# Stick-breaking and differential attention on one core: V and gate columns of the stick-breaking heads computed by seven products ahead of attention, heads reordered and overlapped

## The chip, the core and the metric

The kernel runs on one core of a Trainium2 chip. A core has a matrix engine (TensorE, PE in the profile; PEld is its weight load, which overlaps the products), a vector engine (VectorE, DVE), an activation engine (ScalarE, ACT), GpSimd (POOL) and SyncE (SP), which mostly issues transfers. Each engine runs its own instructions in order and waits for others by semaphores. Operands lie in SBUF (128 partitions), results of TensorE in PSUM. The metric is the device time of one execution in microseconds (us).

## The reference

One layer over 1024 tokens of 2048 features, batch 1:

```python
hn = rmsnorm(h, norm_mix_g[i])
proj = hn @ w_in[i]                              # 2048 x 8192
sb_q, sb_k, sb_v, sb_g, df_q, df_k, df_v, df_g = jnp.split(proj, split_at, axis=-1)
# 8 stick-breaking heads of 128, per query block:
z = q @ k.T * scale;  mask = kpos < qpos
log_not_beta = where(mask, -softplus(z), 0)
later = cumsum(log_not_beta, reverse=True) - log_not_beta
w = where(mask, exp(log_sigmoid(z) + later), 0);  sb_out = w @ v
# 8 differential heads: two 64-wide q/k pairs with partial rotary, one V of 128
a = softmax1 - lam * softmax2;  df_out = rmsnorm(a @ v) * (1 - lambda_init)
mixed = concatenate([sb_out * silu(sb_g), df_out * silu(df_g)])
h = h + mixed @ w_out[i]
gate = sigmoid(rmsnorm(h, norm_ple_g[i]) @ w_ple_gate[i])
h = h + gate * (p[i] @ w_ple_proj[i])
return rmsnorm(h, norm_final_g)
```

All of it is float32, and every product in the kernel keeps nearly float32 precision by three products of rounded halves (fp32r): high by high, high by low, low by high (lines L220, L221, L222).

## The kernel before

Activations lie transposed: features on the 128 partitions, tokens along the free dimension, in reversed order, so that a causal row is a contiguous range and the reverse cumulative product of stick-breaking becomes a forward scan (L313). The tokens are worked in two halves of 512, `half` 1 first (the earlier tokens, whose queries see only that half's keys), then half 0, whose queries see the keys of both. K and V of half 1 go to DRAM (`k_d`, `v_d`) and come back in half 0.

**A unit.** `unit(X)` multiplies two blocks of 128 columns of `w_in` with 16 feature tiles of the half: 2 x 16 x 3 = 96 matmuls of 128x512, into two PSUM tiles `acc`. Its weights come in four pieces; for each, ACT writes the high part (`whi`, L150) and DVE the low part (`wlo`, L151), two pieces deep. A head needs two units: q and k, then V and gate. So half 1 has 32 units, half 0 too.

**The order of the work.** TensorE's instructions are ordered by hand. A head's attention is cut into steps with due times, and `Side.tick()`, called after each group of three matmuls (32 ticks to a unit), issues the steps that are due between the matmuls of the units that follow. Thus attention of one head lies in the units of the next one. The steps of a stick-breaking head: `weights(rb)` for four blocks of 128 queries (scores on TensorE, mask on DVE L300, two sigmoids on ACT L311 and L312, scan L313 and product L314 on DVE, which give the weights `bt`); `values` (transposes of V, `vps`, L336); then, for two pairs of query blocks, `turn` (transposes of the weights into `tp`, L352, split into `awh` on ACT L364 and `awl` on DVE L365) and `mix` (weights by V into `av`, L380 to L385, reduced at L390 and L391). The order of ACT and DVE is chosen by the framework's scheduler in the heads; in the seven-product stage it is written by hand as well.

**PSUM.** Tag "t" has two buffers for `tp`, `vps`, `av` and the small norm sums; tag "acc" two; tag "z" two buffers of two banks for scores.

**The order of heads.** In half 1 the stick-breaking heads 0 to 7 come first, then the differential heads 8 to 15; in half 0 it is the other way around. At a change of kind ACT loads another table of functions. The sums of squares for half 1's norm are made during the first unit, those for half 0 during heads 1 to 4.

**After attention.** The product with `w_out` is made for both halves together by seven products in place of eight (a Strassen form in Winograd's order): operands A11, A12, S2, S1, S3, S4, A22 are sums of quarter matrices. On the activation side the sums S1 to S4 are made while heads finish (`comb_d`, by DMAs that add); on the weight side DVE makes differences `T` (L841) and ACT and DVE split them. Each product is 12 matmuls, 112 products in all. Then come the gate of the per-layer embedding and the final norm.

Of the kernel before, what the change touches and what calls it, by code (L numbers as in the profile page):

```python
# [28 lines left out]
ORDER1 = [*range(16)]  # L29
ORDER0 = [*range(8, 16), *range(8)]  # L30
# [3 lines left out]
GAPS, GAPD = 5, 6  # L34
LATS = 12, 14
# [11 lines left out]
def _body(ctx, nc, tc, ap):  # L47
# [25 lines left out]

    qzs = [const.tile([P, 2, HALF], F32R, name=f"qz{i}", tag=f"qz{i}") for i in range(2)]
# [67 lines left out]
    KT = [2 * pc + k2 + 8 * kh for pc in range(4) for k2 in range(2) for kh in range(2)]  # L142

# [84 lines left out]
    comb_d = dram.tile([2, 4, 4, P, HALF], F32, name="comb_d", tag="comb_d")  # L228
    h_d = dram.tile([2, NK, P, HALF], F32, name="h_d", tag="h_d")
# [34 lines left out]
    def attention(at, pz, half, hd, q, qz, K, KL, VV, sg, vf):  # L264
# [38 lines left out]
        def weights(rb, c):  # L303
# [116 lines left out]
        n1 = n0 - 1  # L420
        if sb:
# [7 lines left out]
        steps = [(t, partial(weights, rb, c)) for rb, ts in enumerate((s0, s1, s2, s3)) for c, t in enumerate(ts)]  # L429
        steps.append((s1[-1] + 2, values))  # L430
        for pr, t, n in ((0, t0, n0), (1, t1, n1)):
# [5 lines left out]
            if not sb:  # L437
                steps.append((t + gap * n + NORM_LAT, partial(norm, pr)))
        return steps

    with tc.tile_pool(name="at", bufs=2) as at, tc.tile_pool(name="pz", bufs=2, space=PSUM) as pz:
        SWAP = [i + 8 if i < 8 else i - 8 if i < 16 else i for i in range(32)]
        rstds = {}
        man = tc.manual_schedule(engines={T.engine})
        man.__enter__()
        for half in (1, 0):
            tsl = slice(half * HALF, half * HALF + HALF)
            X = {}
            if half == 1:
                A.preload_act_table_set("natural_log_exp_and_others")  # L450
                rest_of_w = stream.prep(by_halves=True)
                xs = []
                for i in range(8):
                    if i and i % 2 == 0:
                        stream.prep()
                    kts = KT[2 * i:2 * i + 2]
                    x2 = at.tile([P, 2, HALF], F32, name="x2", tag=("bt", "pt", "k2", "v2")[i % 4], bufs=(3, 2, 2, 2)[i % 4])
                    src = ap["xT"].rearrange("(a k p) t -> k p a t", a=2, p=P)[kts[0], :, :, tsl]
                    if i == 0:
                        for j in range(2):  # L460
                            nc.sync.dma_start(x2[:, j, :], src[:, j, :])
                        rest_of_w()
                    elif i < 4:
                        nc.sync.dma_start(x2, src)
                    else:
                        with tc.issue_after(lastw[0].ins):
                            nc.sync.dma_start(x2, src)
                    for j in range(2):
                        kt = kts[j]
                        X[kt] = split_scaled(kt, x2[:, j, :], gvec[:, 0, kt:kt + 1])  # L470
                        xs.append(x2[:, j, :])
# [6 lines left out]
            if half == 0:  # L478
                G.dma_start(cs, ap["rope"][:, :, tsl])

            for hd in (ORDER0, ORDER1)[half]:
# [5 lines left out]
                if half == 1 and hd == H + 1:  # L487
# [4 lines left out]
                if half == 1 and hd == 0:  # L492
                    pinx = lastx[0]

                    def first_rstd():
                        ss = SumSq(ev, "ssq")
                        for t in xs[:4]:
                            ss.add(t)
                        pa = lastadd[0].ins
                        with tc.issue_after(pa):  # L500
                            G.dma_start(subg, ap["subg"])
                            G.dma_start(lamv, ap["lamv"])
                            G.dma_start(ident, ap["ident"])
                            G.dma_start(masks, ap["masks"])
                        with tc.issue_after(pinx.ins):
                            for i, t in enumerate(xs[4:]):
                                ss.add(t, eng=V if i % 2 else G)
                        with tc.issue_after(pa):
                            G.dma_start(cs, ap["rope"][:, :, HALF:])
                        rstds[1] = ss.rstd(ev, "rstd1")  # L510
                        consts_late()

                    side.add([(18, first_rstd)])
                    za = pz.tile([P, 2, HALF], F32, name="za", tag="z")
                    acc2 = unit(X, acc=[za[:, 0, :], za[:, 1, :]])
# [436 lines left out]
        for _ in range(4):  # L952
            whigh()
            if len(wmade) > 1:
                wlow()
# [277 lines left out]
```

## Time and profile before

| | |
|---|---|
| time, median of 3 runs | 2491.33 us (2490.79 to 2498.24) |
| the profiled execution's own time | 2490.08 us |
| its span, first to last instruction | 2488.2 us |
| granted TensorE clock, mean | 0.994 |
| PE / DVE / ACT / POOL busy | 2440.0 / 1637.2 / 1168.7 / 264.8 us |
| matmuls of 128x512 at L220 to L222 | 2432 at each line with `acc` as the target |
| weight splits | L150 on ACT 332.4 us, L151 on DVE 395.1 us |
| DMA | 350.46 MB, 141 GB/s in the mean |

How to read it: busy times of different engines overlap, and an idle engine costs nothing unless the chain that ends last runs through it. A row of a group shows line, engine, operation, the tile written, the tiles read, shape and count, then busy time, mean ns of one, and idle time of the engine ahead of it with what ended that idle time. A row of a timeline shows start, duration, engine, line, operation; what stands in brackets is the idle time ahead of it and its releaser. The duration of a matmul (0.39 us) is longer than the step from one to the next, since they are pipelined. A window's row shows what each engine was busy in that stretch.

### The profile page before, as it was taken

What the parts mean: (1) busy time and instruction counts of PE and PEld (TensorE: products, weight loads), DVE (VectorE), ACT (ScalarE), POOL (GpSimd) and SP (SyncE); (2) the same over time, 40 slices, a digit from 0 to 9 for tenths busy, and PEclk for the clock granted to TensorE, in tenths of its full rate; (3) what the DMA queues carried; (4) which work ended last, traced back from release to release, by engine and by line L of the source; (5) the groups of instructions that cost most, each with busy time, mean ns of one, the idle gap of its engine ahead of it and who ended that gap; (6) DMA issues with size and microseconds to landing.
All of it is one profiled execution on the core that took longest, in us unless ns stands there. A gap on an engine that the chain in (4) does not pass through costs nothing.

```text
span 2488.2 us, 31261 instructions
## 1 busy us (share of the span) xinstructions
PE 2440.0 (98%) x11626; PEld 2035.9 (82%) x11626; DVE 1637.2 (66%) x2687; ACT 1168.7 (47%) x1936; POOL 264.8 (11%) x295
## 2 busy tenths in 40 slices
PE   8999999999999999999999999999899999999997
PEld 7888888888887888888887888888787887787886
DVE  6554556677778888888876555567568674546555
ACT  6333333455556655555555333435424224546443
POOL 3111000000000000100000000000111113330110
PEclk9999999999999999999999999999999999999999
DMA  5445333444346434454443333436647777343433
GB/s 191 144 142 171 117 112 113 150 136 148 123 127 187 129 114 130 129 133 134 132 119 110 110 111 112 124 112 186 220 161 223 167 188 231 119 132 104 132 109 102
DMA packets 137720, 350.46 MB, mean 141 GB/s; under 512 B 14752, under 2 KB 18848, under 8 KB 137568
## 3 DMA queue, kind: packets, MB, share of 16 engines
q1 hardware_dynamic: 108336, 277.94, 34.9%
q0 software_dynamic: 29232, 70.53, 11.8%
q8 instruction: 91, 1.49, 0.2%
q14 instruction: 61, 0.50, 0.1%
HBM read 272.92 MB, written 83.89 MB: 143 GB/s over the span
## 4 chain that ended last, share of the span: by engine, by line
PE 91%; DVE 4%; ACT 2%; DMA 2%; issue 1%; SPq 0%; DVEq 0%; ACTq 0%
PE acc L220 21%; PE acc L221 21%; PE acc L222 21%; PE tp L352 2%; PE pbc L777 2%; PE pbc L775 2%; PE pbc L776 2%; PE z L294 1%; PE z L293 1%; PE av L385 1%; PE av L384 1%; PE av L383 1%; PE pa L777 1%; PE pa L776 1%; PE pa L775 1%
## 5 line engine op out<-in xcount | busy, mean ns | idle before, releaser
L220 PE MATMUL acc<-xh,whi 128*128 128x512 f32 x2432 | 968.5, 398 | 7.8 <-ACT xh L138 6.3
L221 PE MATMUL acc<-xl,whi 128*128 128x512 f32 x2432 | 950.9, 391 | 0.4 <-DVE xl L139 0.4
L222 PE MATMUL acc<-xh,wlo 128*128 128x512 f32 x2432 | 950.8, 391 | 0.0
L151 DVE TENSOR_TENSOR wlo<-wraw,whi 128x1024 fp32r<-128x1024 f32 (+1 forms) x317 | 395.1, 1246 | 377.8 <-ACT whi L150 366.9
L222 PEld LDWEIGHTS acc<-xh,wlo 128*128 128x128 f32 x2432 | 457.4, 188 | 98.6
L150 ACT CAST whi<-wraw 128x1024 fp32r<-128x1024 f32 (+1 forms) x317 | 332.4, 1049 | 436.5 <-PE acc L221 398.5
L220 PEld LDWEIGHTS acc<-xh,whi 128*128 128x128 f32 x2432 | 458.2, 188 | 94.6 <-ACT xh L138 6.9
L221 PEld LDWEIGHTS acc<-xl,whi 128*128 128x128 f32 x2432 | 458.6, 189 | 86.1 <-DVE xl L139 1.8
L364 ACT CAST awh<-tp 128x256 fp32r<-128x256 f32 (+1 forms) x160 | 80.0, 500 | 180.1 <-PE tp L352 155.8
L365 DVE TENSOR_TENSOR awl<-tp,awh 128x256 fp32r<-128x256 f32 (+1 forms) x160 | 93.1, 582 | 102.8 <-ACT awh L364 101.6
L110 POOL TENSOR_TENSOR ssq<-ssq,sq 128x512 f32<-128x512 f32 x80 | 118.7, 1485 | 379.2 <-ACT sq L109 325.0
L321 ACT ACTIVATE et<-z,mx 128x512 f32<-128x512 f32 (+7 forms) x128 | 94.5, 738 | 55.6 <-DVE mx L318 55.0
L887 ACT CAST wpr<-T 128x512 fp32r<-128x512 f32 x64 | 39.1, 621 | 171.0 <-DVE T L841 170.1
L313 DVE TENSOR_TENSOR_SCAN st<-pt 128x511 f32<-128x511 f32 (+3 forms) x64 | 86.6, 1353 | 20.7 <-ACT pt L311 20.2
L318 DVE TENSOR_REDUCE mx<-z 128x1 f32<-128x512 f32 (+7 forms) x128 | 96.3, 753 | 1.2
L385 PE MATMUL av<-awl,v 128*128 128x256 f32 x256 | 72.8, 284 | 1.6 <-DVE awl L365 1.6
L311 ACT ACTIVATE pt<-z 128x512 f32<-128x512 f32 (+3 forms) x64 | 41.6, 649 | 68.5 <-DVE z L300 68.5
L383 PE MATMUL av<-awh,v 128*128 128x256 f32 x256 | 72.2, 282 | 0.7 <-ACT awh L364 0.7
L384 PE MATMUL av<-awh,v 128*128 128x256 f32 x256 | 72.4, 283 | 0.0
L329 DVE SCALAR_TENSOR_TENSOR et<-et,l 128x512 f32<-128x512 f32 (+3 forms) x64 | 52.0, 813 | 11.5 <-ACT et L328 11.5
L293 PE MATMUL z<-k,q 128*128 128x512 f32 (+2 forms) x160 | 56.6, 358 | 1.3 <-ACT et L321 1.3
L294 PE MATMUL z<-kl,qz 128*128 128x512 f32 (+2 forms) x160 | 57.5, 359 | 0.0
(319 smaller groups left out, 3656.3 us busy)
## 6 DMA issues: line engine op xcount, KB each, us to landing
wraw<-w_in SPq DMA_DIRECT2D x255, 512.0 KB, 3.6
wraw<-w_gate SPq DMA_DIRECT2D x64, 512.0 KB, 3.6
wraw<-w_out SPq DMA_DIRECT2D x56, 256.0 KB, 3.6
comb_d<-sg POOLq DMA_DIRECT2D x48, 256.0 KB, 7.3
k_d<-k POOLq DMA_DIRECT2D x16, 512.0 KB, 4.0
v_d<-v POOLq DMA_DIRECT2D x16, 512.0 KB, 3.6
k<-k_d POOLq DMA_DIRECT2D x16, 512.0 KB, 3.7
v<-v_d POOLq DMA_DIRECT2D x16, 512.0 KB, 4.5
```

Source lines behind the costliest of these rows:

```text
L110: lastadd[0] = eng.tensor_tensor(self.acc, self.acc, s, op=ALU.add)
L150: A.copy(hi[:, o], raw[:, o])
L151: V.tensor_tensor(lo[:, o], raw[:, o], hi[:, o].bitcast(F32), op=ALU.subtract)
L220: T.matmul(acc[c], hi[:, k2, kh, c, :], xh, start=first, stop=False)
L221: T.matmul(acc[c], hi[:, k2, kh, c, :], xl, start=False, stop=False)
L222: T.matmul(acc[c], lo[:, k2, kh, c, :], xh, start=False, stop=last)
L318: V.reduce_max(mx, z[:, vw], axis=AX.X, negate=True)
L321: A.activation(et[:, vw], z[:, vw], AF.Exp, bias=mx[:, 0:1], accum_out=l)
L365: V.tensor_tensor(wl[:, o, :], tp[:, o, :], wh[:, o, :].bitcast(F32), op=ALU.subtract)
L383: T.matmul(av, vv[:, 0, blk % 4, :], wh, start=blk == 2 * pr + 1, stop=False)
L384: T.matmul(av, vv[:, 1, blk % 4, :], wh, start=False, stop=False)
L385: T.matmul(av, vv[:, 0, blk % 4, :], wl, start=False, stop=last)
```

## The change

A new stage ahead of attention computes the V and gate columns of the eight stick-breaking heads, for both halves at once, by the seven-product form that w_out uses: 112 products of 12 matmuls. The code of the w_out stage becomes a class, `Seven`, that both stages use. Unlike in w_out, the activation-side sums are made from x on the chip: four k-tile pairs in place (`combine`, `divide`), four more through DRAM (`visit`, `xcomb_d`). Partial results go through `vgpart_d` and `vghalf_d`; the results stand in `vg_d`. The sums of squares of both halves are made in this stage (`squares`), and the norms follow at the fourth tick of the first unit (`norms`). The split tiles of x for half 1 are reused or loaded from a copy (`load_x1`).

A stick-breaking head then has one unit (q, k). Its V and gate columns are loaded by two DMAs on POOL's queue and scaled. The due times are closer (turns every 4 ticks instead of 5, the second pair of query blocks at tick 32 in half 0 and 28 in half 1), so a head's steps run 40 to 48 ticks, and the last of them fall into the next head's unit of 32 ticks. Both halves take the differential heads first. The last differential head has a tighter set of due times. One of the weight buffers (`bt2`) and the padded q tiles (`qz`) share a tag.

```diff
-ORDER1 = [*range(16)]
-ORDER0 = [*range(8, 16), *range(8)]
+ORDER1 = ORDER0 = [*range(8, 16), *range(8)]
-GAPS, GAPD = 5, 6
-LATS = 12, 14
+GAPS, GAPD = 4, 6
+SECOND = 32, 28
...
-            units = [ap["w_in"][hd][i] for order in (ORDER1, ORDER0) for hd in order for i in range(2)]
+            units = [ap["w_in"][hd][i] for order in (ORDER1, ORDER0) for hd in order for i in range(1 if hd < H else 2)]
...
-                bt = at.tile([P, S], F32, name="bt", tag="bt", bufs=3)
+                if rb == 2:
+                    bt = at.tile([P, S], F32, name="bt2", tag="qz")
+                else:
+                    bt = at.tile([P, S], F32, name="bt", tag="bt", bufs=3)
...
         if sb:
-            s0, s1, s2, t0 = [0], [3], [7], 14
+            ss, t0 = [[0], [3], [7], [11]], 16
+            t1 = SECOND[half]
         else:
-            s0, s1, s2, t0 = [0, 2], [5, 8], [12, 15], 19
-        gap = GAPS if sb else GAPD
-        last = t0 + gap * (n0 - 1)
-        s3 = [last + 1 + 4 * c for c in range(len(s0))]
-        t1 = s3[-1] + (LATS[half] if sb else LATD[half])
+            tight = hd == 2 * H - 1
+            s0, s1, s2, t0 = ([0, 1], [3, 5], [7, 9], 14) if tight else ([0, 2], [5, 8], [12, 15], 19)
+            gap = 3 if tight else gap
+            last = t0 + gap * (n0 - 1)
+            s3 = [last + 1, last + (3 if tight else 5)]
+            ss = [s0, s1, s2, s3]
+            t1 = s3[-1] + (7 if tight else LATD[half])
...
+        gv = Seven(lambda u, ph, k: ap["w_vg"][u, ph, k], H)
...
+        def combine(i):
+            ka, kb = KX[0][i]
+            (a2, b2), (a1, b1) = raw2[i], (raw1[i][:, 0, :], raw1[i][:, 1, :])
+            def one():
+                gv.split("A22", i, *gv.places("A22", i), gain=gcol(kb), raw=b2)
+            def two():
+                A.activation(b2, b2, AF.Copy, scale=gcol(kb))
+                V.scalar_tensor_tensor(b2, a2, gcol(ka), b2, op0=ALU.mult, op1=ALU.add)
+            return [one, two, lambda: V.tensor_tensor(a2, a2, a1, op=ALU.subtract),
+                    lambda: V.scalar_tensor_tensor(a1, a1, gneg[:, ka:ka + 1], b2, op0=ALU.mult, op1=ALU.add),
+                    lambda: V.scalar_tensor_tensor(b1, b1, gneg[:, kb:kb + 1], a1, op0=ALU.mult, op1=ALU.add)]
...
+        def vput(o, ph, hf, blk, u):
+            G.dma_start((vg_d if ph else vghalf_d)[hf, blk, u], o)
...
+        def norms():
+            t = ev.tile([P, HALF], F32, name="ssq", tag="ssq")
+            for hf in (1, 0):
+                ps = pp.tile([P, HALF], F32, name="ssps", tag="t")
+                T.matmul(ps, ones, ssa[hf], start=True, stop=True)
+                rstd_from(ps, 1.0 / NK, eps6, EPS, ssa[hf], t)
+                rstds[hf] = ssa[hf]
+            consts_late()
+        side.add([(4, norms)])
...
                 acc = unit(X)
+                if sb:
+                    vf, gf = f32t("vf"), f32t("gf")
+                    for i, t in enumerate((vf, gf)):
+                        G.dma_start(t, vg_d[half, i, hd])
...
-                    acc = unit(X)
-                vf = f32t("vf")
-                V.tensor_tensor(vf, acc[0], rstd, op=ALU.mult)
-                gf = f32t("gf")
-                V.tensor_tensor(gf, acc[1], rstd, op=ALU.mult)
+                if sb:
+                    vacc = vf, gf
+                else:
+                    vacc = unit(X)
+                    vf, gf = f32t("vf"), f32t("gf")
+                V.tensor_tensor(vf, vacc[0], rstd, op=ALU.mult)
+                V.tensor_tensor(gf, vacc[1], rstd, op=ALU.mult)
```

More of the change, by code (lines that the diff above doesn't have):

```diff
@@ L72, in _body @@
     lam = const.tile([P, 1], F32, name="lam", tag="lam")
-    qzs = [const.tile([P, 2, HALF], F32R, name=f"qz{i}", tag=f"qz{i}") for i in range(2)]
+    qzs = {}
     nqz = [0]
@@ L437, in attention @@
             if not sb:
-                steps.append((t + gap * n + NORM_LAT, partial(norm, pr)))
+                steps.append((t + gap * n + (7 if tight else NORM_LAT), partial(norm, pr)))
         return steps
@@ L449, in _body @@
             if half == 1:
[L450 to L471, printed above, removed]
+                X = X1
             else:
@@ L907, in _body @@
[L907 to L921 removed]
+        op.begin()
@@ L951, in _body @@
         wload(1, 22)
[L952 to L955, printed above, removed]
+        op.lead()
         prev = None
```

587 lines of the change are left out of this document (405 added, 182 removed).

## The prediction

> **What bounds the kernel now.** I read the page first: the span, the busy times, the slices and the chain that ended last.
>
> ```profile
> span 2488.2 us, 31261 instructions
> PE 2440.0 (98%) x11626; PEld 2035.9 (82%) x11626; DVE 1637.2 (66%) x2687; ACT 1168.7 (47%) x1936; POOL 264.8 (11%) x295
> PE   8999999999999999999999999999899999999997
> PE 91%; DVE 4%; ACT 2%; DMA 2%; issue 1%; SPq 0%; DVEq 0%; ACTq 0%
> ```
>
> TensorE (PE) is busy in 98% of the span and carries 91% of the chain. A matmul taken away is worth its time, and a pause put between matmuls costs its time. VectorE (DVE), at 66%, is an average, so I cut windows at the stages the change touches. The columns are window; length, PE busy; weight loads; DVE; ACT; POOL; granted clock; DMA share; GB/s.
>
> ```profile
> 2072.32:2094.04 21.72, 21.72 (x98) 17.98 (x97) 8.95 (x11) 9.12 (x13) 1.28 (x1) 1.00 0.67 224
> 105.10:154.10 49.00, 49.00 (x234) 41.04 (x234) 25.27 (x38) 18.77 (x32) 7.43 (x7) 1.00 0.48 153
> 1443.10:1499.50 56.40, 56.40 (x286) 47.84 (x285) 33.83 (x42) 21.49 (x32) 3.69 (x6) 1.00 0.38 112
> 425.60:450.60 25.00, 23.45 (x105) 18.91 (x104) 14.57 (x25) 10.16 (x16) 2.65 (x4) 1.00 0.56 158
> 1323.90:1360.70 36.80, 33.23 (x174) 27.93 (x173) 24.51 (x33) 20.55 (x30) 3.23 (x5) 1.00 0.39 100
> 0.00:60.00 60.00, 53.35 (x212) 42.14 (x213) 38.18 (x50) 36.24 (x53) 19.58 (x24) 1.00 0.58 190
> 1725.50:2072.30 346.80, 334.47 (x1479) 273.71 (x1478) 241.24 (x369) 122.07 (x211) 49.89 (x70) 0.99 0.71 199
> ```
>
> The first row is one plain unit of 96 products of 128x512 (two neighbours fall in): 21.72/96 gives the 0.2268 us that one more such matmul costs. The next two rows are stick-breaking heads, in half 1 and in half 0: two units each and no idle PE. The fourth and fifth are the two changes of head kind; the sixth is the start. The last is the seven-product stage of w_out: PE pauses for 346.80 − 334.47 = 12.3 us in its 346.8.
>
> **The change, part by part.** *Matmuls.* Eight heads in two halves lose their v,gate unit: 16 x 96 = 1536 products less. The new stage has 7 x 8 x 2 = 112 products of 12, 1344 more. Net −192 x 0.2268 = **−43.5 us**. Of five matmuls with ones, which add up squares for the norms, three stay; two take 1.02 us: −1.
>
> ```profile
> 46.43 1.02 PE L122 MATMUL ssps<-ssq,onesr 128*128 128x512 f32 x2
> v<-v_d POOLq DMA_DIRECT2D x16, 512.0 KB, 4.5
> ```
>
> *The new stage.* It works like the w_out stage, whose window shows 12.3 us of pauses; the start, which the stage replaces, has 60.00 − 53.35 = 6.7. The code differs in one thing: its operands are combined on the chip, so DVE is nearly full through the first A11 and A12 products, and each matmul needs a split operand behind it. Before has no such stretch. Bounds: −3 (half of the start's pauses go) to +14 (the w_out stage's pauses on top of a start 2 us later). I take **+4**: the w_out stage's 12.3, scaled by nothing since it has the same 1344 products, less the 6.7 of the old start, is 5.6, and that stage has transitions in it that the new one lacks. The DMA traffic (weights, combinations and partial sums through DRAM, on SP's and POOL's queues) hides under the 305 us of matmuls in the stage; in w_out 0.71 of the DMA engines carries the like.
>
> *Stick-breaking heads, the start of the scores.* Today the scores follow a whole v,gate unit, so q and k are long ready. After the change they stand three matmuls (and the previous head's mix) behind the end of the q,k unit. What must run first is k's low part, and DVE has the next weights' low part before it:
>
> ```profile
> 1417.15 1.05 ACT L150 CAST whi<-wraw 128x1024 fp32r<-128x1024 f32 x1 [1.43 <-PE acc L221]
> 1417.38 0.69 DVE L531 TENSOR_TENSOR qk<-acc,rstd 128x512 f32<-128x512 f32 x1
> 1418.24 1.23 DVE L151 TENSOR_TENSOR wlo<-wraw,whi 128x1024 fp32r<-128x1024 f32 x1 [0.17 <-ACT whi L150]
> L533 ACT CAST k<-qk 128x512 fp32r<-128x512 f32 x16 | 9.9, 617 | 0.0
> L534 DVE TENSOR_TENSOR k<-qk,k 128x512 fp32r<-128x512 f32 x16 | 10.8, 676 | 0.0
> 1419.22 0.28 PE L383 MATMUL av<-awh,v 128*128 128x256 f32 x1
> 1419.33 0.28 PE L384 MATMUL av<-awh,v 128*128 128x256 f32 x1
> ```
>
> From the unit's end: acc is readable at +0.2, the second qk ends at 0.9, whi at 1.0 on ACT, wlo (1.23) at 2.25, k's low part (0.68) at 2.9. PE is there after 3 x 0.227 and the mix's small products (a step of 0.11 each): 1.5 in half 1 and 1.9 in half 0. So PE waits 1.4 us a head in half 1 and 1.0 in half 0. The steps between matmul starts show 0.3 us of idle in a half-1 head today and 0.6 in a half-0 head, too finely spread for the busy column. So 8 x 1.1 = **+9** for half 1, bounds +2 (ACT and DVE take k ahead of the weights) and +14.
>
> *Half 0, the values step.* This is the large term. In the changed kernel a head's second pair of turns (ticks 32, 36, 40) falls into the next head's ticks 0, 4 and 8. At tick 5 the transposes of V want one of the two PSUM buffers of tag "t". One holds `av` of the older head, the other the `tp` of tick 4, which DVE frees with `awl`. In the order in which DVE's instructions are built, this `awl` stands behind the new head's first two blocks of weights: mask, scan, mask, product, scan, product. The same run of instructions in before, with the work that goes ahead of it:
>
> ```profile
> 1445.86 0.29 DVE L300 TENSOR_TENSOR z<-z,masks 128x128 f32<-128x128 f32 x1
> 1447.24 2.29 DVE L313 TENSOR_TENSOR_SCAN st<-pt 128x1023 f32<-128x1023 f32 x1 [1.09 <-ACT pt L311]
> 1449.44 0.28 DVE L300 TENSOR_TENSOR z<-z,masks 128x128 f32<-128x128 f32 x1
> 1449.63 1.22 DVE L314 TENSOR_TENSOR bt<-st,bt 128x1023 f32<-128x1023 f32 x1
> 1450.78 2.01 DVE L313 TENSOR_TENSOR_SCAN st<-pt 128x895 f32<-128x895 f32 x1
> 1452.89 1.09 DVE L314 TENSOR_TENSOR bt<-st,bt 128x895 f32<-128x895 f32 x1
> L391 DVE TENSOR_REDUCE sm<-av 128x128 f32<-128x384 f32 x64 | 35.3, 551 | 4.5 <-ACT sm L390 4.5
> L559 DVE TENSOR_TENSOR vf<-acc,rstd 128x512 f32<-128x512 f32 x31 | 21.3, 687 | 4.7 <-PE acc L222 4.3
> L365 DVE TENSOR_TENSOR awl<-tp,awh 128x512 fp32r<-128x512 f32 x96 | 66.0, 688 | 86.3 <-ACT awh L364 85.4
> L365 DVE TENSOR_TENSOR awl<-tp,awh 128x256 fp32r<-128x256 f32 x64 | 27.0, 422 | 16.5 <-ACT awh L364 16.2
> ```
>
> From the first mask to the last product is 1453.98 − 1445.86 = 8.1 us. After k's low part (2.9) DVE first does the reduce 0.55, lead 0.29 (as a mask, of its size), vf 0.69, sg 0.42 (as the small awl), gf 0.69 and the small awl 0.42; the next starts some 0.1 before one ends (1449.63 in 1449.44 + 0.28), so the first mask starts at 5.4. Then 5.4 + 8.1 = 13.5, and the wide awl (0.69) is done at 14.1. PE reaches the transposes after 18 unit products (4.1), the scores of two blocks (2.6: nine products of 512 columns and three of 384), av, tp and mix (2.0: some 18 small ones at 0.11) and the wait of 1.0: 9.7. It stands **4.4 us**. Behind the waiting transposes stands the whole rest of the unit. With the 1.0 from above, less the 0.6 of small idle a head has today: 8 x 4.8 = **+38**. Bounds: +15 (DVE's order does better by 3 us: the six instructions ahead of the mask hide under the wait for k) and +48 (a further wait at tick 12, for the awl of block 2, which by the same rows comes within 0.5 us of PE).
>
> *The clock.* A gap of this length in a PE that otherwise never rests has a price of its own:
>
> ```profile
> 1743.11:1746.52 3.41, 1.37 (x5) 0.84 (x6) 3.31 (x5) 2.82 (x6) 1.13 (x2) 1.00 0.20 77
> 1746.52:1749.94 3.42, 3.42 (x10) 2.66 (x9) 0.97 (x2) 0.00 (x0) 0.00 (x0) 0.50 0.79 220
> 1797.72:1801.13 3.41, 1.47 (x6) 0.57 (x4) 2.61 (x5) 1.80 (x4) 0.00 (x0) 1.00 0.77 264
> 1801.13:1807.96 6.83, 6.11 (x14) 4.79 (x15) 5.05 (x9) 1.53 (x3) 0.54 (x1) 0.50 0.25 78
> ```
>
> Twice in w_out a stretch of 3.41 us with about 2 us of idle PE (3.41 − 1.37 and 3.41 − 1.47) is followed by half the clock, once for 3.42 us and once for 6.83, which costs 1.7 and 3.4 us of matmuls. A gap of 4.4 always puts at least 2.2 into one such stretch. I take seven heads (the eighth lies beside the w_out products) at the lower price: 7 x 1.7 = **+12**; bounds 0 and 8 x 3.4 = +27.
> The Trainium skill, "TensorE: Matmul & The Clock Gate", section "Why this matters for your kernels", speaks against such a gap: it asks for none above about 3 us, since one idle window takes the clock back to half. By that rule each head pays, and the sum is as above. The traced rows agree, and show the drop after a window of 3.41 us that was idle for 2.
>
> *Changes of head kind.* Differential to stick-breaking now comes in both halves, as the dearer of the two: 3.6 us of idle PE (36.80 − 33.23) against 1.6 (25.00 − 23.45), both at full clock: +2, and as an estimate half as much again for the extra activation tables. **+3**, bounds −3 and +10. The loads of V and gate (two DMAs of 256 KB a head on POOL's queue) can start when the older head's vf is transposed, over 20 us ahead of their use, against a landing of 4.5 us for twice the size (the `v<-v_d` row): nothing; were they late, the vf ahead of the first mask would be, and the values step with it.
>
> Sum: −43.5 − 1 + 4 + 9 + 38 + 12 + 3 = +21.5, on the profiled execution's 2490.08 us: **2511**. The median of the runs is 2491.33, 1 us higher, which the range swallows.
>
> **The rivals.** *Other side: the values step is not late.* If DVE has the wide awl done when PE comes at 9.7 (4.4 us sooner: k's low part and the six instructions would have to be done when the scores come), the term is 8 x 0.4 = 3 and the clock stays: −43.5 − 1 + 4 + 9 + 3 + 3 = −25.5, **2465**. It decides once the stall is under some 2 us, where no clock is lost either (−25.5 + 8 x 2 = −9.5). For it: the head in half 0 has no visible idle today (56.40 of 56.40). Against it: today a whole unit lies between the q,k unit and the scores, and no older head's turns beside them.
> *The gaps are there but the clock holds.* The change of kind above has 3.6 us idle, spread, at 1.00. Then the 12 us of clock go: **2499**, at the edge of no change.
> *The new stage starves.* DVE is full there and each product waits for an operand. At w_out's rate of pauses doubled (25 us over the 305 us of matmuls, less the 6.7 of the start) and a dropped clock at three of them, about +18 in place of +4: **2525**.
> *The overlap doesn't pay at all:* DVE becomes the bound of half 0. A short head there needs 33.83 − 4 x 1.23 = 28.9 us of DVE, in 56.40 − 21.72 = 34.7 us of PE: close, but not the bound, and worth no more than the waits above.
> The Trainium skill, "Perfetto Trace Analysis", section "Optimization Strategy", takes consistent bubbles as a sign that PSUM has no room for the next tile; no run here shows yet that it is so.
>
> **How the numbers follow.** About 0.3% (7.5 us) is what a measurement of this kernel can tell from no change. The forecast with its clock loss 0.45, the gaps without it 0.18, the starved stage 0.13, the values step in time 0.20, something else 0.04. The forecast's own range is 2503 to 2527. The 8-in-10 range leaves out the upper tail of the starved stage (0.06) and the larger part of the fast rival (0.12), and so runs from 3 us above that rival to 2530: 2468 to 2530. Faster by over 0.3%: the fast rival, with a little of the rest, 0.22. Within: half of the gaps without clock, 0.12. Slower: 0.66.
>
> **What would show it.** Right: half-0 stick-breaking heads of 38 to 42 us instead of 34.7, their V transposes with 4 us of idle ahead, released by `awl`; the clock below 1 once a head; scores in half 1 waiting 1.4 us for DVE's k; seven-product matmuls 448 to 896 groups of three. Wrong: heads of 34 to 36 us in half 0, clock 0.99 and more, or a new stage far over 310 us.

## The result and the profile after

| | before | after |
|---|---|---|
| time, median | 2493.87 us (4 runs) | 2561.61 us (2559.24 to 2569.24, 4 runs) |
| ratio to before | | 1.0276, 95% interval 1.0247 to 1.0304 |
| profiled execution, span | 2490.08, 2488.2 us | 2559.24, 2557.4 us |
| granted clock, mean | 0.994 | 0.983 |

The change costs 68 us. The prediction had the direction and 20 us of it; its range ended at 2530. Runs of one kernel lie up to 10 us apart, so a difference of a few us between two medians is not told apart here; for such differences the windows of the traces are read. The page of the kernel after:

```profile
span 2557.4 us, 31930 instructions
PE 2433.3 (95%) x11434; PEld 2016.1 (79%) x11434; DVE 1799.4 (70%) x3009; ACT 1219.4 (48%) x2065; POOL 298.1 (12%) x393
PE   7999999999999999999999988888899999999997
PE 75%; issue 9%; DVE 8%; ACT 3%; DMA 3%; POOL 1%; SPq 0%; DVEq 0%; POOLq 0%; ACTq 0%
```

The 192 matmuls are gone (11626 to 11434), but TensorE's share of the chain that ends last fell from 91% to 75%, and the row of slices has a dent of eights from the 24th to the 29th slice. The dent is half 0's short heads. Windows of the kernel after, in the order of the stages (columns as in the prediction; PE busy is the second time):

```profile
0.00:339.50 339.50, 314.45 (x1344) 253.93 (x1345) 263.11 (x407) 138.21 (x236) 50.79 (x99) 0.99 0.75 249
796.90:941.00 144.10, 139.06 (x687) 115.29 (x686) 98.64 (x171) 61.35 (x121) 12.68 (x22) 1.00 0.52 161
941.00:1008.30 67.30, 60.75 (x276) 49.55 (x275) 49.50 (x85) 33.52 (x63) 6.75 (x10) 0.92 0.63 184
1524.40:1734.30 209.90, 185.31 (x947) 156.70 (x947) 143.19 (x190) 88.38 (x137) 24.44 (x35) 0.94 0.43 113
1734.30:1782.40 48.10, 39.48 (x190) 32.27 (x189) 36.05 (x51) 24.49 (x41) 3.23 (x4) 0.93 0.60 165
1782.40:2140.00 357.60, 338.36 (x1508) 277.70 (x1507) 245.82 (x378) 125.38 (x218) 50.02 (x70) 0.98 0.69 193
```

They are the new stage, five short heads of half 1 (28.8 us each), the switch of halves, five short heads of half 0 (42.0 each), the last unit, which makes q and k of the eighth head and holds the steps of the seventh, and the w_out stage with the steps of the eighth. To see where the time came from, I took for every step from one matmul's start to the next what it exceeds its steady length (0.227 us for 512 columns, 0.12 for 256, 0.11 for 128), which counts idle time and half clock together, and the time ahead of the first matmul:

| part (before against after) | before | after | more | forecast |
|---|---|---|---|---|
| start and first two units / start and new stage | 12.3 | 34.2 | +21.9 | +4 |
| rest of half 1 with the switch of halves | 14.2 | 33.3 | +19.1 | +9 and some of the 3 |
| differential heads of half 0 | 5.6 | 4.8 | −0.8 | 0 |
| half 0: change of kind, first six short heads | 8.8 | 58.2 | +49.4 | +39 (6 x 4.8 and 6 x 1.7) and the rest of the 3 |
| last unit and w_out, which hold the steps of the last short head before, of the last two after | 21.7 | 42.4 | +20.7 | +11 (2 x 4.8 and 1.7) |
| gate and end | 15.7 | 17.1 | +1.4 | 0 |

Together +111.7; less 192 x 0.2268 = 43.5 this is +68.2, against 2557.4 − 2488.2 = 69.2 in the spans.

The large wait is where the prediction put it. TensorE's rows with a wait in one short head of half 0, whose unit starts at 1566.8, and the waits of the transposes of V in the whole execution (us in total, times, longest):

```profile
1569.76 0.50 PE L293 MATMUL z<-k,q 128*128 128x512 f32 x1 [0.82 <-DVE k L975]
1580.95 1.10 PE L342 MATMUL vps<-ident,vf 128*128 128x128 f32 x4 [4.06 <-DVE awl L371]
```

```profile
PE vps L342 <- DVE awl L371: 32.3, 8, 5.1
```

DVE ahead of them, in the same head:

```profile
1571.83 0.42 DVE L371 TENSOR_TENSOR awl<-tp,awh 128x256 fp32r<-128x256 f32 x1
1572.16 0.29 DVE L303 TENSOR_TENSOR z<-z,masks 128x128 f32<-128x128 f32 x1
1572.61 0.69 DVE L1009 TENSOR_TENSOR sg<-sg,gf 128x512 f32<-128x512 f32 x1 [0.16 <-ACT sg L1004]
1573.55 2.29 DVE L319 TENSOR_TENSOR_SCAN st<-pt 128x1023 f32<-128x1023 f32 x1 [0.24 <-ACT pt L317]
1575.75 0.28 DVE L303 TENSOR_TENSOR z<-z,masks 128x128 f32<-128x128 f32 x1
1575.94 1.23 DVE L320 TENSOR_TENSOR bt<-st,bt 128x1023 f32<-128x1023 f32 x1
1577.09 2.02 DVE L319 TENSOR_TENSOR_SCAN st<-pt 128x895 f32<-128x895 f32 x1
1579.20 1.09 DVE L320 TENSOR_TENSOR bt<-st,bt 128x895 f32<-128x895 f32 x1
1580.21 0.68 DVE L371 TENSOR_TENSOR awl<-tp,awh 128x512 fp32r<-128x512 f32 x1
```

The wide `awl` that frees the buffer is done at 1580.9, 14.1 us behind the start of the unit (forecast: 14.1), and the wait is 4.06 (forecast: 4.4). The eight heads of half 0 wait 32.3 us in sum. DVE's order is the one read from the built program, but that the product for `sg` comes behind the first mask and not ahead of it. The windows around this gap show the clock:

```profile
1574.00:1577.58 3.58, 2.89 (x18) 2.20 (x16) 3.58 (x4) 1.95 (x3) 0.00 (x0) 1.00 0.00 0
1577.60:1581.00 3.40, 0.05 (x1) 0.05 (x1) 3.19 (x3) 0.67 (x2) 0.00 (x0) 1.00 0.00 0
1581.01:1584.41 3.40, 3.40 (x11) 2.83 (x11) 0.69 (x1) 0.78 (x2) 0.00 (x0) 0.50 0.00 0
```

A stretch of 3.4 us with 0.05 us of work, then 3.4 us at half clock.

### The profile page after: what moved, and what is told of

The parts are those of the page before. It is cut to its first block, busy times and chain, and to the rows that moved or that the text cites. A ratio compares the mean times of both kernels' runs of the same rounds, so it can differ in the third digit from the quotient of the medians.

```text
span 2557.4 us, 31930 instructions
## 1 busy us (share of the span) xinstructions
PE 2433.3 (95%) x11434; PEld 2016.1 (79%) x11434; DVE 1799.4 (70%) x3009; ACT 1219.4 (48%) x2065; POOL 298.1 (12%) x393
## 4 chain that ended last, share of the span: by engine, by line
PE 75%; issue 9%; DVE 8%; ACT 3%; DMA 3%; POOL 1%; SPq 0%; DVEq 0%; POOLq 0%; ACTq 0%
PE acc L218 15%; PE acc L219 15%; PE acc L220 15%; PE pbc L510 3%; PE pbc L512 3%; PE pbc L511 3%; PE tp L358 2%; DVE st L319 1%; PE pa L510 1%; PE pa L511 1%; PE pa L512 1%; PE z L297 1%; PE z L296 1%; PE av L391 1%; PE av L390 1%
## 5 line engine op out<-in xcount | busy, mean ns | idle before, releaser
L218 PE MATMUL acc<-xh,whi 128*128 128x512 f32 x1568 | 633.1, 404 | 1.5 <-DVE gt L1136 1.5
L220 PE MATMUL acc<-xh,wlo 128*128 128x512 f32 x1568 | 617.1, 394 | 0.0
L219 PE MATMUL acc<-xl,whi 128*128 128x512 f32 x1568 | 617.0, 393 | 0.0
L149 DVE TENSOR_TENSOR wlo<-wraw,whi 128x1024 fp32r<-128x1024 f32 x252 | 312.8, 1242 | 268.4 <-ACT whi L148 264.0
L148 ACT CAST whi<-wraw 128x1024 fp32r<-128x1024 f32 x252 | 265.2, 1052 | 325.1 <-PE acc L219 294.7
L220 PEld LDWEIGHTS acc<-xh,wlo 128*128 128x128 f32 x1568 | 297.3, 190 | 65.1
L218 PEld LDWEIGHTS acc<-xh,whi 128*128 128x128 f32 x1568 | 298.4, 190 | 58.0 <-issue 2.4
L219 PEld LDWEIGHTS acc<-xl,whi 128*128 128x128 f32 x1568 | 298.8, 191 | 55.4 <-issue 0.5
L510 PE MATMUL pbc<-cS,wpr 128*128 128x512 f32 x224 | 88.0, 393 | 5.5 <-DVE u L1276 4.2
L608 DVE TENSOR_TENSOR wpr<-T,wpr 128x512 fp32r<-128x512 f32 x128 | 87.7, 685 | 3.4 <-ACT wpr L594 1.5
L511 PE MATMUL pbc<-cS,wpr 128*128 128x512 f32 x224 | 87.6, 391 | 0.0
L512 PE MATMUL pbc<-cS,wpr 128*128 128x512 f32 x224 | 87.6, 391 | 0.0
```

Source lines behind the costliest of these rows:

```text
L148: A.copy(hi[:, o], raw[:, o])
L149: V.tensor_tensor(lo[:, o], raw[:, o], hi[:, o].bitcast(F32), op=ALU.subtract)
L218: T.matmul(acc[c], hi[:, k2, kh, c, :], xh, start=first, stop=False)
L219: T.matmul(acc[c], hi[:, k2, kh, c, :], xl, start=False, stop=False)
L220: T.matmul(acc[c], lo[:, k2, kh, c, :], xh, start=False, stop=last)
L510: T.matmul(o, wh[:, w], xh, start=start and k == 0, stop=False, skip_group_check=True)
```

## The experiments

All but where said are the changed kernel with one edit; times are medians, ratios are to the kernel before.

**The V transposes later.**

```diff
-        steps.append((ss[1][-1] + 2, values))
+        steps.append((13 if sb and half == 0 else ss[1][-1] + 2, values))
```

> One number changed: in half 0 the V transposes of a stick-breaking head are due at tick 13, after the older head's last mix, in place of tick 5. Theory (PE stands 4.1 to 5.1 us a head at these transposes, since both PSUM buffers of their tag wait for DVE): the wait at the transposes goes, and the next to wait is the mix at tick 8, for the same low part of the turned weights, about 1.4 us later than PE; so some 3 us a head and most of the clock loss (1.7 us a head) come back, a short head of half 0 goes from 41.6 to about 37.5 us and the time from 2561.6 to about 2525. Rival (DVE itself has no time left in these heads, and PSUM is only where it shows): the same wait moves to the mix at tick 8, the heads stay at 41 us and the time above 2555.

Measured: 2529.39 us (1.0149, 1.0134 to 1.0164), 32 less. A window of four short heads of half 0, and TensorE's rows with a wait in the first:

```profile
1561.60:1712.00 150.40, 141.90 (x757) 120.03 (x756) 113.56 (x152) 68.62 (x108) 19.52 (x28) 1.00 0.46 126
```

```profile
1564.51 0.50 PE L293 MATMUL z<-k,q 128*128 128x512 f32 x1 [0.82 <-DVE k L975]
1575.70 0.39 PE L391 MATMUL av<-awl,v 128*128 128x256 f32 x1 [0.71 <-DVE awl L371]
1581.39 0.38 PE L391 MATMUL av<-awl,v 128*128 128x256 f32 x1 [0.57 <-DVE awl L371]
```

A head takes 150.4/4 = 37.6 us, the clock is 1.00, and what is left of the wait stands at the mix, as the theory had it, with 0.7 in place of 1.4. DVE does the same work in a shorter time (113.6 of 150.4 us), so it was not the bound; a buffer held behind DVE's order was.

**Work in the gap.** Ahead of the transposes stand matmuls that nobody needs.

```diff
...
+            if sb and half == 0 and hd < H - 1:
+                fill = pz.tile([P, S], F32, name="fill", tag="z")
+                xh = X[KT[0]][0]
+                for i in range(18):
+                    T.matmul(fill[:, 0:HALF], xh[:, 0:P], xh, start=i == 0, stop=i == 17)
             vps = pp.tile([P, 4, P], F32, name="vps", tag="t")
```

> Ahead of the V transposes of seven heads of half 0 stand 18 matmuls of 128x512 whose product nobody reads (18 x 0.227 = 4.1 us, written to a free PSUM tile). They do nothing but keep TensorE at work in the gap. Theory (the gap drops the clock, and this costs 1.7 us or more a head beside the gap itself): the added work lies wholly in the gap, the granted clock of half 0's short heads goes from 0.94 to nearly 1.00, and the time falls by 10 to 17 us, to about 2548, although 126 matmuls are added. Rival (the lower clock is hidden behind the waits on DVE, so it costs nothing): the time stays within 4 us of 2561.6 or rises.

Measured: 2551.37 us (1.0240, 1.0223 to 1.0257): 10 us less with 126 matmuls more. Five short heads of half 0:

```profile
1526.70:1728.00 201.30, 197.09 (x1036) 166.28 (x1035) 142.88 (x190) 88.10 (x136) 24.40 (x35) 1.00 0.43 118
```

The same five took 209.90 us at a clock of 0.94. What the added work can have helped is the clock: its fall costs (209.9 − 201.3)/5 = 1.7 us a head, the forecast's price.

**The scores spread out instead.**

```diff
-            ss, t0 = [[0], [3], [7], [11]], 16
+            ss, t0 = ([[0], [5], [9], [13]] if half == 0 else [[0], [3], [7], [11]]), 16
```

with the transposes at tick 13 as above.

> In half 0 the scores of a stick-breaking head are due at ticks 0, 5, 9, 13 in place of 0, 3, 7, 11, and the V transposes at 13. So the older head's turn at tick 4 is built ahead of the second block's scan, and on DVE the wide low part stands behind one scan and not behind two. Theory (it is the place of this instruction in DVE's order that makes PE wait): neither the transposes nor the mix at tick 8 wait any more; a short head of half 0 goes from 41.6 to 35.5 to 36.5 us, the clock there to 1.00 but for the changes of head kind, the time to about 2515. Rival (DVE's total is the bound in these heads): heads of 39 us or more, time above 2545.

Measured: 2542.64 us (1.0203, 1.0188 to 1.0218). Four short heads of half 0, and a wait of the first:

```profile
1563.70:1719.80 156.10, 146.07 (x757) 122.37 (x756) 114.33 (x152) 68.64 (x109) 19.53 (x28) 0.98 0.45 122
```

```profile
1590.54 0.50 PE L386 MATMUL av<-lead,v 128*128 128x256 f32 x2 [1.68 <-DVE lead L364]
```

39.0 us a head, between theory and rival. The old wait is gone, but the fourth block's scan now comes two ticks later, the lead tile of the new head's own first turn stands on DVE behind it and the next weights' low part, and TensorE waits there; in two of these four heads the clock fell too. Moving instructions moves the wait along DVE's order.

**All steps two ticks later.** The edit of the first experiment (at tick 15) and

```diff
-            ss, t0 = [[0], [3], [7], [11]], 16
-            t1 = SECOND[half]
+            ss, t0 = [[2], [5], [9], [13]], 18
+            t1 = SECOND[half] + 2
```

> On top of the V transposes at a later tick (15 in half 0), every step of a stick-breaking head is due two ticks later in both halves, so six more matmuls (1.36 us) stand ahead of the first scores. Theory (the scores wait 1.0 to 1.2 us a head for k's low part, and only that): short heads of half 1 go from 28.8 to 27.6 us, of half 0 from 37.6 to 36.5, and the time from 2529.4 to 2510 to 2516. Rival (DVE only hands the same lateness on to the turns): the heads keep their length within 0.3 us and the time stays above 2525.

Measured: 2502.92 us (1.0047, 1.0032 to 1.0062), 26.5 less than the first experiment, more than expected. Four heads of half 0 and five of half 1:

```profile
1548.70:1693.60 144.90, 140.92 (x758) 120.07 (x757) 112.06 (x152) 67.83 (x109) 19.50 (x28) 1.00 0.48 131
797.80:936.80 139.00, 138.90 (x686) 115.26 (x685) 98.77 (x171) 59.57 (x120) 12.63 (x22) 1.00 0.52 167
```

36.2 us a head (from 37.6) and 27.8 (from 28.8): 8 x 1.4 + 8 x 1.0 = 19 us. The scores no longer wait for k: in the changed kernel these waits are 17 us in sum (12.4 for DVE's part, 4.7 for ACT's). The other 7.5 are not told apart by this run; the first short head of half 0 fell from 44.2 to 38.3 us and the last unit with the w_out part by 5. With 59 of the 68 us back by due times alone, the waits in the short heads are the main cause of the loss.

**The order of heads undone in half 1.**

```diff
-ORDER1 = ORDER0 = [*range(8, 16), *range(8)]
+ORDER1 = [*range(16)]
+ORDER0 = [*range(8, 16), *range(8)]
...
-            tight = hd == 2 * H - 1
+            tight = half == 0 and hd == 2 * H - 1
```

and the choice of tables that belongs to it.

> The order of heads alone goes back to that of before: in half 1 the stick-breaking heads first, in half 0 the differential ones first. So the switch of halves lies between two differential heads again, and half 1 has the cheaper change of kind, as before. Theory (the switch behind a short head costs 12.7 us of idle and slow steps, the change of kind in half 1 another 6.4, against 5.5 and 2.5 in before): the time falls by 8 to 13 us against 2561.6. Rival (the splitting of half 0's x, 16 tiles on ACT and DVE, is what the switch waits for, whatever head stands there): the time falls by under 4 us.

Measured: 2554.41 us (1.0260, 1.0243 to 1.0277), 7 less: just under the theory's range, above the rival's. The size is loose, since the runs (2550.6 to 2560.3) overlap those of the changed kernel (2559.2 to 2569.2). The changed kernel's switch of halves has waits of the last short head's weights:

```profile
962.38 0.51 PE L386 MATMUL av<-lead,v 128*128 128x256 f32 x2 [2.04 <-DVE lead L364]
...
980.58 0.58 PE L391 MATMUL av<-awl,v 128*128 128x256 f32 x1 [1.42 <-DVE awl L371]
```

With the old order the switch takes as long as before the change. The window of this run, and that of the kernel before:

```profile
945.20:1001.00 55.80, 51.46 (x243) 42.01 (x242) 48.37 (x102) 37.83 (x73) 5.37 (x8) 1.00 0.57 189
```

```profile
779.20:834.90 55.70, 51.51 (x243) 42.07 (x242) 48.34 (x102) 37.95 (x73) 4.46 (x7) 1.00 0.61 189
```

The 16 tiles of half 0's x are split on ACT and DVE at this place in either order. Behind a short head, whose steps leave DVE no slack, they make TensorE wait, and twice the clock falls (0.92 in the window).

**The new stage's start.** On ACT and DVE the first splits of x go behind the two small pieces of weights.

```diff
...
-        gv.first(0, parts, xloads)
-        for i in range(4):
-            split1(0, i)
...
+        gv.first(0, parts, xloads, two_splits)    # two splits of x behind each piece
```

> In the new stage's start the splits of the first four x tiles are put, on ACT and DVE, right behind the two small pieces of weights, ahead of the third piece of 256 KB. Theory (the first matmul comes at 11.3 us and not at 6.3 because ACT, in the order written by hand, waits until 10.04 for a piece of weights that is needed much later): the first matmul comes at 5.5 to 7 us, and the time falls by 3 to 5 us. Rival (the transfers are the limit, 390 GB/s): the first matmul comes earlier, the next ones wait for the third and fourth x tile, and the time falls by under 1.5 us.

Measured: 2561.73 us (1.0279, 1.0263 to 1.0294): nothing. The time is the rival's; its reason, the transfers, is put to the test further down. The first matmul before the change, in the changed kernel, and TensorE's first waits in this run:

```profile
6.27 0.79 PE L220 MATMUL acc<-xh,whi 128*128 128x512 f32 x1 [6.27 <-ACT xh L138]
```

```profile
11.34 0.80 PE L510 MATMUL pa<-cA11h,wfh 128*128 128x512 f32 x1 [11.34 <-ACT cA11h L501]
```

```profile
6.18 0.80 PE L510 MATMUL pa<-cA11h,wfh 128*128 128x512 f32 x1 [6.18 <-ACT cA11h L501]
10.05 0.79 PE L510 MATMUL pa<-cA11h,wfh 128*128 128x512 f32 x1 [0.58 <-ACT cA11h L501]
23.22 0.50 PE L510 MATMUL pa<-cA11h,wfh 128*128 128x512 f32 x1 [0.76 <-ACT wfh L530]
24.48 0.50 PE L512 MATMUL pa<-cA11h,wfl 128*128 128x512 f32 x1 [0.53 <-DVE wfl L531]
...
38.09 0.50 PE L510 MATMUL pa<-cA11h,wfh 128*128 128x512 f32 x1 [1.50 <-ACT wfh L530]
```

The first matmul comes 5.2 us sooner (6.18 against 11.34), and by 66.3 us the lead is gone, for the most part in waits for weights. The stage ends at 339.5 us in both.

**Less work on DVE in the stage, first part.** On the version with the early start, S1 to S4 of the first four pairs use their high part twice.

```diff
         def divide(nm, i):
+            ...                       # ACT writes hi, as before
+            gv.XC[nm, i] = hi, hi     # no low part on DVE
+            return
```

> In the new stage the operands S1 to S4 of the first four k-tile pairs are used with their high part in both places; their 16 low parts are not computed on DVE (16 x 0.69 = 11 us of its work). The number of matmuls stays. It stands on the kernel whose first matmul comes at 6.2 us. Theory (up to the first S products DVE is the limit: it was busy 14.7 of 16.3 us there and TensorE waits for weight splits behind this work): the stage ends 5 to 10 us sooner than 339.5 us. Rival (the transfers at 390 GB/s in the first 36 us, or ACT, set the pace): the stage ends at most 2 us sooner.

Measured: the stage ends at 340.1 us, the time is 2562.33 (1.0284, 1.0263 to 1.0304). The theory falls: 11 us of DVE less, nothing gained.

**Loads held back.** On the version with the early start; `pin[0]` is the load of a partial result in a product of the stage, and what is held back is issued behind it:

```diff
-                nc.sync.dma_start(raw, xsrc(*src))
+                with tc.issue_after(pin[0].ins):
+                    nc.sync.dma_start(raw, xsrc(*src))
...
-                    nc.sync.dma_start(h_d[1, KT[8 + u]], xsrc(1, KT[8 + u]))
+                    with tc.issue_after(pin[0].ins):
+                        nc.sync.dma_start(h_d[1, KT[8 + u]], xsrc(1, KT[8 + u]))
```

> On the kernel whose first matmul comes at 6.2 us, twelve loads of 256 KB that depend on nothing (four of x, eight copies of x from DRAM to DRAM for later use) are held back on SP's queue until the part of the new stage that needs them; in the kernel after the change the scheduler had put them ahead of the weights of the first products. Theory (in the stage's first 40 us TensorE waits for weights that land late, since these 3 MB share 390 GB/s with them): the waits at 22 and 36 us go, the earlier start is kept, and the stage ends at 331 to 334 us in place of 339.5; the time is 5 to 8 us below 2561.6. Rival (ACT and DVE set the pace of the stage's first part, the transfers are hidden): the stage ends within 2 us of 339.5.

Measured: the stage ends at 339.1 us; 2558.31 (1.0256, 1.0240 to 1.0271). The longest wait for weights in the first 40 us (1.50 above) goes, and the first part ends 2 us sooner. From 12 to 36 us the DMA engines were full with the early start alone (share 1.04) and are not here (0.74), and yet TensorE is as busy as before, 21.9 of 24 us; so its other waits there are not for the sum of the transfers:

```profile
12.00:36.00 24.00, 21.87 (x87) 15.91 (x86) 14.44 (x21) 13.43 (x21) 3.80 (x7) 1.00 1.04 387
```

```profile
12.00:36.00 24.00, 21.85 (x87) 15.91 (x86) 14.43 (x21) 14.11 (x22) 3.80 (x7) 1.00 0.74 271
```

Then the 2 us are lost to the clock. One gap of 2.7 us is in both kernels; here it lies in a single stretch:

```profile
126.72:130.13 3.41, 0.90 (x4) 0.67 (x4) 3.38 (x6) 1.03 (x2) 0.54 (x1) 1.00 0.88 282
130.13:133.55 3.42, 3.42 (x10) 2.67 (x9) 1.88 (x4) 1.15 (x2) 0.54 (x1) 0.50 1.04 350
```

and in the changed kernel, 2 us later against stretches that begin elsewhere, it is split between two and costs no clock:

```profile
126.93:130.34 3.41, 2.04 (x10) 1.31 (x8) 2.64 (x5) 2.37 (x4) 0.02 (x1) 1.00 0.94 276
130.34:133.75 3.41, 2.27 (x10) 1.87 (x11) 3.38 (x6) 0.28 (x1) 1.08 (x2) 1.00 0.99 344
```

**Much less work on DVE in the stage.** On the version with the late copies, S1 to S4 of the first pairs without low parts (as above), the sums of `visit` left out (what is stored is unsummed), and each square written in place of being added.

```diff
-                V.scalar_tensor_tensor(b2, a2, gcol(ka), b2, op0=ALU.mult, op1=ALU.add)
                 store("S1", b2)
...
-                        A.activation(ts[j], ts[j], AF.Square)
-                        V.tensor_tensor(ssa[j % 2], ssa[j % 2], ts[j], op=ALU.add)
+                        A.activation(ssa[j % 2], ts[j], AF.Square, scale=4.0)
```

> On the version with the early start and the late copies, DVE loses most of what the new stage has beyond the w_out stage: the low parts of S1 to S4 of the first four pairs (the high part stands in both places), the four sums of each of the other four pairs (the parts of x are stored unsummed) and the adding of squares (each square replaces the one before it). That is some 60 instructions and 43 us of DVE's 262 us in the stage; matmuls and transfers stay. Theory (the waits inside the stage, about 12 us and two drops of the clock behind the first S products, are for DVE's sum of work): they shrink by more than half and the stage ends at 328 to 333 us in place of 339.1. Rival (each is the wait for one operand that is late by its place in the order, or by ACT or a transfer, as in the w_out stage): the stage ends at 336 us or later.

Measured: the stage ends at 343.3 us, 4 later; the time is 2556.73 (1.0258, 1.0206 to 1.0310, two runs), not told apart from that of the version with the late copies. The switch of halves behind it took 64.6 us here in place of 67.3, with one fall of the clock and not two. The window of its stage:

```profile
0.00:343.30 343.30, 318.67 (x1345) 254.60 (x1346) 226.97 (x349) 136.04 (x233) 52.65 (x101) 0.99 0.73 247
```

DVE has 36 us less than in the changed kernel and the stage is no shorter: some old waits went, a new one of 3.5 us came at 74.6 us for a weight difference T that DVE makes late, for a reason the profile does not name. So the stage is not bound by DVE's sum of work. Which order of loads, splits and products would close its some twenty gaps was not found, and stays open.

**All edits together**: the late copies and early start, the old order in half 1, the later steps.

> All together: the earlier start, the loads held back, half 1's old order of heads, the V transposes at tick 15 of half 0 and all steps of the short heads two ticks later. If the gains add up (14 + 42 + 5 to 8 for the stage, 7 for the order and 59 for the ticks, from 2561.6): 2488 to 2496 us, no different from the kernel before (2491). If the stage's part is given back again: 2496 to 2500. So the seven products' 43.5 us would be paid away by the start of the new stage, the changes of head kind and the waits that stay.

Measured: 2498.30 us (1.0020, 1.0011 to 1.0029). (The expectation names 14 + 42 beside the 59 of which they are parts.) From the single runs 2561.6 − 58.7 − 7.2 − 3.3 = 2492.4 would follow; the 6 us between are within what the smaller two of these gains leave open. The largest wait in the w_out stage, and what DVE waited for ahead of it:

```profile
1802.77 0.77 PE L511 MATMUL pbc<-cS,wpr 128*128 128x512 f32 x1 [6.96 <-DVE u L1288]
```

```profile
1801.93 0.69 DVE L1288 TENSOR_TENSOR u<-pbc,s 128x512 f32<-128x512 f32 x1 [3.68 <-DMA s<-part_d]
```

This wait was 4.21 us in the changed kernel. It ends with a transfer: DVE itself stands idle for 3.68 us until a partial sum is back from DRAM. The last short head now ends two ticks later; whether this makes the wait longer is what the next version tries.

**The last head faster**, and eight splits of the new stage two products later, on top:

```diff
+            if half == 0 and hd == H - 1:
+                ss, t0, gap, t1 = [[2], [5], [8], [11]], 16, 3, 28
...
-                    gv.xq.extend((gv.slot + 3, load_x(nm, u - 3)) for nm in ("A11", "A12"))
+                    gv.xq.extend((gv.slot + 5, load_x(nm, u - 3)) for nm in ("A11", "A12"))
```

> On the version with all edits together, two more due times: the last short head of half 0, which has no head after it, turns every 3 ticks and ends 9 ticks sooner; and in the new stage eight splits of x come two products later, away from the sums of x that stand in the same place. Theory (TensorE stands 7.1 us in the w_out stage for an operand that the last head hands over late, and 2.7 us with 1.7 us of half clock in the new stage for DVE): 7 to 10 us come back, and the time is 2488 to 2492 us, at or just below the kernel before. Rival (both waits are for DVE's sum of work and only move): 2496 us or more.

Measured: 2496.82 us (1.0020, 1.0011 to 1.0029): the rival. The wait of 7 us falls to 1.65, so the end of that head sets most of it. But the closer turns of the same head wait in its place, 4.10 us where the version with all edits had at most 0.5, and so does one turn of the head before it (1.91):

```profile
1714.76 0.58 PE L390 MATMUL av<-awh,v 128*128 128x256 f32 x1 [1.91 <-ACT awh L371]
1759.35 0.58 PE L390 MATMUL av<-awh,v 128*128 128x256 f32 x1 [4.10 <-ACT awh L371]
1803.44 0.47 PE L513 MATMUL pbc<-cS,wpr 128*128 128x512 f32 x1 [1.65 <-DVE u L1290]
```

In the new stage the wait near 129 us is gone, yet the stage ends at 338.5 us, from 339.1.

No version that was run beats the kernel before.

## Why the prediction was wrong

*Right.* The direction, and the mechanism in the short heads. Matmuls: 192 less, −43.5, as the counts show (21.72/96 is 0.2263 and not 0.2268, which moves the term by 0.1). The scores' wait for k: 28.8 us a head in half 1 (forecast 27.3 + 1.1 = 28.4); moving the steps took 1.0 us a head away there and 1.4 in half 0. The values step: 4.06 against 4.4, released by the instruction that was named; the run with later transposes took 42.0 − 37.6 = 4.4 us from each head, its share of the clock among them. The clock: 1.7 us a head, shown by the added matmuls. A short head in the middle of half 0 takes 42.0 us against 34.7 + 4.8 + 1.7 = 41.2 forecast. The Trainium skill, "TensorE: Matmul & The Clock Gate", section "Why this matters for your kernels", warns of gaps above about 3 us; the run with work in the gap agrees (10 us), and here a gap of 2.7 us was enough where it lay in a single stretch. The Trainium skill, "Perfetto Trace Analysis", section "Optimization Strategy", says that consistent bubbles can mean a lack of room in PSUM; here that reading holds for 8 waits of 32.3 us in sum, all for a buffer of one tag, and a later due time removed them with no more PSUM.

*Wrong: the new stage, "I take +4".* This is the step that failed. It measured +21.9, beyond the bound of +14. The sum took w_out's 12.3 us of pauses and subtracted the old start's 6.7. But 6.27 of these 6.7 are the time ahead of the first matmul, and the sum put the new stage's own such time at nothing; it is 11.34. In the prediction's own column the new stage stands 339.50 − 314.45 = 25.05 us, 11.34 ahead of the first matmul and 13.7 behind it. So the comparison with w_out nearly held for the inside (13.7 against 12.3), and 12.3 + 11.3 − 6.7 = 17 would have been near the 18.4 that this column shows. The other 3.5 us up to 21.9 are half clock and short waits, which a busy column does not show.

That the late first matmul alone sets the stage's length is not so: with the early start the same time came back as waits inside. What sets it stays open. The reason that the prediction gave for bounds and rival, DVE nearly full, fell by two runs, and the sum of the early transfers by one. The rival of a starved stage was nearer, at +18, and its own terms (25 − 6.7 and three falls of the clock at 1.7) give 23; but this was luck, since 11.3 of its 25 us are one wait at the start and not a wait for each product.

*Wrong: "Changes of head kind, +3".* The term held the change of tables and left out the switch of halves, with its 16 splits of x behind a head that now has no slack. By the steps between starts the switch cost 12.7 us against 5.5 in before, and half 1's change of kind 6.4 against 2.5. Some 7 us came back with the old order.

*Too small: the heads at the edges.* The sum priced eight equal heads, the eighth without its clock. The five in the middle of half 0 came near it, with 209.9 − 5 x 34.7 = 36.4 us against 5 x 6.5 = 32.5. But the first, behind a differential head, takes 47.0 us (1477.4 to 1524.4), and the last unit, with the seventh head's steps, 48.1. The last two heads together cost +20.7 and not 11: by the steps, some 13 in the last unit and 8 in the w_out stage. In that unit waits at the turns (1.69 us for `lead`, 1.04 for `awl`) come on top of the values step. No run takes these heads away; the last two versions show that the last head's ticks decide where the waits stand, not what the part would be without them.

Each of these three lies in a place where two kinds of work meet, and the range took them as small.

## What to carry to other kernels

Work that is made shorter to save matmuls must keep its support engines' order in step: read in the built program what stands ahead of the instruction that frees a PSUM buffer, and place the next user behind it; here two due times were worth 59 us, more than the 43.5 us of matmuls that the whole change saved. Before one stage is taken as the model of another, count the time ahead of the first matmul by itself, and measure the pauses inside by the steps between matmul starts; the busy column hid 3.5 us here. A gap that leaves less than 1.5 us of matmuls in one stretch of 3.41 us is to be priced with its half clock, 1.7 us and more.

## What the runs showed of the hardware

Work without use can pay: 126 matmuls more made the kernel 10 us faster, since they kept the clock (1.00 in place of 0.94 over five heads).

The clock is judged in fixed stretches of 3.41 us, and not gap by gap: the gap of 2.7 us cost a stretch of half clock where it lay in one stretch (0.90 us of work left in 3.41) and none where two stretches shared it (2.04 and 2.27 us of work). In each of the 13 traces all falls to half clock begin on one grid of 3.413 us, which lies at another place of the span from run to run. Between the first and the last matmul, a stretch at full clock with less than 1.5 us of busy PE was always followed by half clock, and one with 2.0 us or more never was; from 1.5 to 1.96 us both occur. So a kernel that becomes 2 us faster ahead of such a gap can lose 1.7 us at it, as the version with the late copies did.
